# A hybrid layer on one core: no products with the zero state, and another order at both ends

## The chip, the core and the metric

The kernel runs on one core of a Trainium2 chip. The metric is the device time of one execution in microseconds. TensorE (PE) multiplies matrices, VectorE (DVE), ScalarE (ACT) and GpSimd (POOL) do the elementwise work, and SyncE (SP) issues most of the DMAs. Each engine works through its own instructions in the order in which they were written into its program, and waits on semaphores for the others. A difference of some 0.2% (2.6 us) is about what runs of this kernel can tell from none.

## The reference

One layer over 1024 frames of width 1024, in float32:

```
u = RMSNorm(h);  p = u @ W_in                      # q,k,v of attention; q,k,v, gate, decay, beta of the DeltaNet
A = chunked band attention (8 heads of 64)
B = gated DeltaNet (4 heads of 128), a recurrence over chunks:
      v_new = val - kc @ S
      o     = qd @ S + att @ v_new
      S     = S * cd + kt^T @ v_new                # S starts at zero
h = h + concat[RMSNorm(A), B] @ W_out
h = h + relu(RMSNorm(h) @ W1)^2 @ W2
```

S is the state. In the first chunk both products with S are zero and S times its decay is zero too. After the last chunk nothing reads S any more.

## The kernel before

Every float32 matrix is split into a high and a low part in a format that PE multiplies faster (line 147 casts the high part on ACT, line 148 subtracts it on DVE or POOL), and a product is three products of the parts.

The stages follow one another on PE: the projections of the DeltaNet (0 to about 235 us), of attention (to about 363), then attention together with the recurrence (to about 575), the output projection (to about 662), and the two layers of the feed-forward part, ff1 (to about 970) and ff2 (to 1281).

*The start.* GpSimd writes a matrix of ones. PE multiplies it with itself WARM times (line 111, tile warm), which is work for nothing but to keep PE busy. Meanwhile x and the gains (mgain) arrive. `load_xt` (lines 176 to 196) makes the high part uh of x times its gain on ACT (line 185), the low part ul on DVE (186), and squares x on ACT (190, 192) for the norm. ACT has to load a table before its first ACTIVATE, and the load stands in ACT's order just ahead of that instruction. `load_w` fetches the weights wdk of the first product, dk, and splits them.

*The recurrence.* The frames are eight chunks of 128 (c = 0 to 7), and each piece of a chunk is a generator that gives up its turn at every `yield`: `delta_prep` solves the triangular system and writes k with its tail decay (kt) to DRAM; `delta_state` forms tpv (v turned), pk (k times the state), pv (the new values vn), pq (q times the state, o) and pS (the update of the state); `delta_out` forms tpq, mt, po and the norm of o, whose reciprocal root is a chain of small operations on POOL (lines 131 to 143, with the power at 133); `delta_fin` turns o (tpo) and writes it, times the gate, into a quarter buffer mixd. Four-product groups go through `four` (line 461), turns through `four_t` (465). The state alternates between two tiles, the first of which is set to zero on POOL (line 231).

`interleave` mixes these pieces with the units of attention by weights, and the framework's planner then puts each engine's instructions into an order by priority and by its own estimate of times; buffers come from pools, and who gets one depends on that order. So the program order at one place can change when instructions are taken out at another.

*ff2.* The product of f and W2 is made with seven products in place of eight per block, in four blocks kb. Each product is 48 matmuls: `product` splits two operands of two tiles each (four splits on DVE), PE multiplies, and `accumulate` adds the result out of PSUM into one of seven sums y1 to y7 on DVE (line 1251), or copies it on ACT in the first block. The `prep` functions form sums and differences of operands on DVE in place, so their order matters. In the last block (`last`) the sums are also merged into the four quarters of the output (line 1255, on POOL or DVE), which `store` sends out. The very last product is made by rows (`by_rows`), so that each of its four results can be subtracted (line 1310) and sent out as soon as it is done; a row takes six matmuls with the first pair of operand tiles and then six with the second.

Of the kernel before, what the change touches and what calls it, by code (L numbers as in the profile page):

```python
# [8 lines left out]
F32 = mybir.dt.float32  # L9
F32R = mybir.dt.float32r  # L10
AF = mybir.ActivationFunctionType
# [24 lines left out]
ORDER = "OSMOSMFSOMOSMSL"  # L36
LATE = 2
SPREAD = 5
WARM = 8
LAST = {"b22": "t1", "t3": "t2", "t4": "b22"}  # L40
RS = "a"
NV = 6
# [4 lines left out]
def hymba_kernel(  # L47
# [53 lines left out]
    def bank(pool, name):  # L101
        return pool.tile([P, 512], F32, tag="bk", name=name)
# [3 lines left out]

    ones = cpool.tile([P, P], F32, name="ones")
    nc.gpsimd.memset(ones, 1.0)
    warm = bank(ps_o, "warm")
    for i in range(WARM):  # L110
        nc.tensor.matmul(warm[:, 0:P], ones, ones, start=True, stop=True)
# [64 lines left out]
    def load_xt(hf, k):  # L176

        raw = page("dk", f"xt{hf}{k}")
        if not hf and not k:
            nc.scalar.dma_start(out=raw, in_=x_t[0, :, 0:TH])  # L180
            nc.sync.dma_start(out=mgain, in_=mix_gain)
        else:
            nc.sync.dma_start(out=raw, in_=x_t[k, :, hf * TH:(hf + 1) * TH])
        hi, lo = u[hf][k]
        nc.scalar.mul(hi, raw, mgain[:, k:k + 1])
        nc.vector.scalar_tensor_tensor(lo, raw, mgain[:, k:k + 1], hi.bitcast(F32), ALU.mult, ALU.subtract)
        acc = squares[hf][k % 2]
        if acc is None:
            squares[hf][k % 2] = acc = page("pp", f"xs{hf}{k}")
            nc.scalar.activation(acc, raw, AF.Square)  # L190
        else:
            nc.scalar.activation(raw, raw, AF.Square)
            (nc.gpsimd if k % 2 else nc.vector).tensor_tensor(acc, acc, raw, ALU.add)

    for k in range(NKT):
        if k:
            w_dk.append(load_w(w_in[k * P:(k + 1) * P, DK:DK + 512], f"wdk_{k}"))
        load_xt(0, k)
        if not k:
            w_dk.append(load_w(w_in[0:P, DK:DK + 512], "wdk_0"))  # L200

    def row_load(src, w, name):
        t = mpool.tile([P, w], F32, name=name)
# [24 lines left out]
    split(wab, wab2[:, :, 0:8], wab2[:, :, 8:16], nc.scalar, nc.vector)  # L228

    state = [mpool.tile([P, 4, P], F32, name=f"state{i}") for i in range(2)]  # L230
    nc.gpsimd.memset(state[0], 0.0)

    q_dr = dram.tile([NT, 64, 2, 2, 512], F32, name="q_dr")
    k_dr = dram.tile([4, 2, P, SEQ], F32, name="k_dr")
# [256 lines left out]
    def delta_prep(kT, ab):  # L491
# [4 lines left out]
        for c in range(NT):  # L496
            n = f"d{c}"
            h4 = slice(4 * c, 4 * c + 4)
            tp = bank(ps_d, n + "_tp")
            four_t(tp, head(kT[c]))  # L500
            ss = sumsq(page("pp", n + "_sq"), "p", tp, n)
            kt = page("pp", n + "_kt")
            nc.vector.tensor_tensor(b4(kt), b4(tp), bc_row(ab["edec"][:, 1, h4]), ALU.mult)
            nc.sync.dma_start(out=kt_dr[c], in_=kt)
            yield 500
            L = decay("pp", n + "_L", ab, h4, tri_s, tri_ur, nc.vector)
            r = rsqrt("p", ss, 4, 1.0, EPS, n)
# [13 lines left out]
            nc.sync.dma_start(out=a_dr[c], in_=A)  # L521
            yield 900
# [74 lines left out]

    def delta_state(c, ab, kTs, Ys, D):

        n = f"c{c}"  # L600
        T = "wh" if c + 1 < NT else "jv"
        h4 = slice(4 * c, 4 * c + 4)
# [12 lines left out]
        pk = bank(ps_d, n + "_pk")  # L615
        four(pk, lambda h, hs: kT[:, hs], lambda h, hs: S[:, h, :])
        for h in range(4):
            hs = slice(h * P, (h + 1) * P)
            nc.vector.scalar_tensor_tensor(
                rr[:, hs], pk[:, hs], ab["nbr"][:, 4 * c + h:4 * c + h + 1], rr[:, hs],  # L620
                ALU.mult, ALU.add)
        yield 900
# [6 lines left out]
        pq = bank(ps_d, n + "_pq")  # L629
        four(pq, lambda h, hs: dq[:, hs], lambda h, hs: S[:, h, :])  # L630
        o = page("cv", n + "_o")
        nc.vector.tensor_tensor(b4(o), b4(pq), bc_row(ab["edec"][:, 0, h4]), ALU.mult)
        yield 900
        pS = bank(ps_d, n + "_pS")
        four(pS, lambda h, hs: ktail[:, hs], lambda h, hs: vn[:, hs])
        for h in range(4):
            nc.vector.scalar_tensor_tensor(
                S2[:, h, :], S[:, h, :], ab["edec"][:, 2, 4 * c + h:4 * c + h + 1],
                pS[:, h * P:(h + 1) * P], ALU.mult, ALU.add)
        D[c] = dq, dg, vn, o  # L640
        yield 900

    def delta_out(c, ab, kTs, D):
# [23 lines left out]
        nc.vector.tensor_tensor(o, o, po, ALU.add)  # L667
# [491 lines left out]
    def ff2(psw, pools):  # L1159
# [52 lines left out]
        for kb in range(nb):  # L1212
# [69 lines left out]

            accumulate(1, product(f"p1{kb}", lambda i: (a11[i], b11[i])))
            accumulate(5, product(f"p5{kb}", prep5))
            accumulate(2, product(f"p2{kb}", lambda i: (a12[i], b21[i])))
            if last:
                merge(nc.gpsimd, 2, 1)
                store(y[2], 0, 0)
            accumulate(3, product(f"p3{kb}", prep3))
            accumulate(6, product(f"p6{kb}", prep6))  # L1290
            if last:
                merge(nc.vector, 6, 1)
                merge(nc.gpsimd, 3, 5)
                for m in range(2):
                    nc.gpsimd.tensor_tensor(y[5][m], y[5][m], h11[m], ALU.add)
# [112 lines left out]
```

## Time and profile before

| | |
|---|---|
| time, median of 3 runs | 1288.59 us (1287.44 to 1289.28) |
| the profiled execution, its own time | 1288.31 us |
| its span | 1286.6 us |
| PE busy | 1260.6 us |
| DVE, ACT, POOL busy | 935.0, 553.9, 293.0 us |
| first product starts, last product ends | 6.30 us, about 1281.4 us |

The span is the time between the first and the last instruction that the profile shows; the execution takes 1.7 us more. In the profile a row gives the start, the duration, the engine, the line, the operation and the tiles, and in brackets how long the engine had been idle and whom it had waited for. A row of the view by groups gives the count, then the busy time, the mean of one in ns and the idle time ahead of them.

### The profile page before, as it was taken

How to read it: one execution, taken by the hardware profiler on the slowest of the kernel's cores; microseconds unless marked ns; L12 is line 12 of the kernel's file. 1: busy time of each engine (PE TensorE's matmuls, PEld its weight loads, DVE VectorE, ACT ScalarE, POOL GpSimd, SP SyncE). 2: the span in 40 equal slices, each digit the busy share in tenths (PEclk: the TensorE clock that was granted, in tenths of full speed). 3: DMA queues.
4: the chain of work that ended last, by engine and by line, in shares of the span. 5: the costliest groups of instructions: out<-in, count | busy, mean ns of one | idle time of the engine just before them, and what ended most of it. 6: DMA issues, size and time to landing. Idle time of an engine off the chain costs nothing.

```text
span 1286.6 us, 18043 instructions
## 1 busy us (share of the span) xinstructions
PE 1260.6 (98%) x6702; PEld 1040.6 (81%) x6702; DVE 935.0 (73%) x1401; ACT 553.9 (43%) x919; POOL 293.0 (23%) x499
## 2 busy tenths in 40 slices
PE   9999999999999999989999999999999999999998
PEld 7778878788888887868877788888887888888886
DVE  7899987665046666863529876776668997897988
ACT  7233132133166664665335445444455443333331
POOL 4435461454024355523310000000000000000034
PEclk9999999999999999999999999999999999999999
DMA  6214353656492742125351433232358733422002
GB/s 223 61 44 140 100 164 112 145 147 160 144 270 79 218 109 75 42 65 163 122 166 31 151 116 129 98 110 97 105 196 318 238 93 104 131 86 95 17 33 98
DMA packets 129288, 160.65 MB, mean 125 GB/s; under 512 B 22832, under 2 KB 71984, under 8 KB 128688
## 3 DMA queue, kind: packets, MB, share of 16 engines
q1 hardware_dynamic: 111104, 137.20, 34.7%
q10 hardware_dynamic: 18096, 22.29, 5.0%
q8 instruction: 53, 0.87, 0.3%
q14 instruction: 35, 0.29, 0.1%
HBM read 111.75 MB, written 47.71 MB: 124 GB/s over the span
## 4 chain that ended last, share of the span: by engine, by line
PE 72%; DVE 8%; issue 2%; DMA 2%; POOL 1%; ACT 1%; POOLq 1%; SPq 0%; ACTq 0%; DVEq 0%
PE q L1087 22%; PE p L1183 20%; PE op L166 5%; PE av_ps L166 3%; PE aq_ps L166 3%; PE g_ps L166 3%; PE t_o L865 3%; PE ak_ps L166 2%; PE t_sb L793 1%; PE t_sa L793 1%; PE t_tpb L844 1%; PE t_tpa L855 1%; PE c_mt L461 1%; PE c_pS L461 1%; DVE ml L148 1%
## 5 line engine op out<-in xcount | busy, mean ns | idle before, releaser
L1255 POOL TENSOR_TENSOR y<-y,y 128x1024 f32<-128x1024 f32 x6 | 19.3, 3243 | 591.7 <-DVE y L1251 572.9
L1251 DVE TENSOR_TENSOR y<-y,p 128x1024 f32<-128x1024 f32 x46 | 55.2, 1218 | 5.4 <-PE p L1183 4.5
L808 DVE CUSTOM_DVE_ANT_0 t_pb<-t_sb,biasn 128x256 f32<-128x256 f32 (+1 forms) x64 | 25.4, 402 | 43.6 <-POOL biasn L720 25.4
L166 PE MATMUL op<-mh,wo_h 128*128 128x512 f32 x128 | 50.3, 393 | 0.8 <-DVE t_nm L808 0.3
L166 PE MATMUL op<-ml,wo_h 128*128 128x512 f32 x128 | 50.1, 391 | 0.0
L166 PE MATMUL op<-mh,wo_l 128*128 128x512 f32 x128 | 48.3, 391 | 0.0
L823 ACT ACTIVATE t_pb<-t_pb,t_nm 128x256 f32<-128x256 f32 (+1 forms) x64 | 31.6, 494 | 22.7 <-DVE t_nm L817 12.7
L966 DVE TENSOR_TENSOR h<-op,op_x 128x512 f32<-128x512 f32 x16 | 10.8, 688 | 30.7 <-PE op L166 30.7
L793 PE MATMUL t_sb<-ks,t_q 128*128 128x256 f32 (+1 forms) x144 | 30.4, 308 | 0.8 <-DMA t_q<-q_dr 0.5
L973 POOL TENSOR_TENSOR op_q<-op_q 128x512 f32<-128x512 f32 x14 | 20.1, 1439 | 48.0 <-ACT op_q L972 47.8
L166 PEld LDWEIGHTS op<-mh,wo_h 128*128 128x128 f32 x128 | 24.0, 188 | 7.4 <-issue 1.0
L817 DVE CUSTOM_DVE_ANT_0 t_pa<-t_sa,biaso,t_nm 128x384 f32<-128x384 f32 (+2 forms) x48 | 26.3, 547 | 4.4 <-PE t_sa L793 2.9
L865 PE MATMUL t_o<-t_ta,vt 128*64 128x128 f32 x240 | 27.3, 293 | 1.4 <-DVE t_ta L858 1.1
L166 PEld LDWEIGHTS op<-mh,wo_l 128*128 128x128 f32 x128 | 24.0, 188 | 5.2 <-issue 0.2
L166 PEld LDWEIGHTS op<-ml,wo_h 128*128 128x128 f32 x128 | 24.0, 188 | 4.9
L166 PE MATMUL g_ps<-uh,wg_h 128*128 128x512 f32 x64 | 25.2, 394 | 1.4 <-ACT wg_h L147 1.4
L826 ACT ACTIVATE t_pa<-t_pa,t_nm 128x384 f32<-128x384 f32 (+2 forms) x48 | 26.4, 550 | 0.1
L793 PE MATMUL t_sa<-ks,t_q 128*128 128x256 f32 (+2 forms) x128 | 25.5, 310 | 0.3 <-DVE t_nm L808 0.3
L166 PE MATMUL g_ps<-uh,wg_l 128*128 128x512 f32 x64 | 25.2, 394 | 0.4 <-POOL wg_l L148 0.4
L166 PE MATMUL dq_ps<-uh,wdq_h 128*128 128x512 f32 x64 | 25.5, 398 | 0.0
L166 PE MATMUL dv_ps<-uh,wdv_l 128*128 128x512 f32 x64 | 25.4, 397 | 0.0
L166 PE MATMUL aq_ps<-waq_h,uh 128*128 128x512 f32 x64 | 25.3, 401 | 0.0
(1102 smaller groups left out, 4353.8 us busy)
## 6 DMA issues: line engine op xcount, KB each, us to landing
wa<-in_w_ff_dram SPq DMA_DIRECT2D x32, 512.0 KB
a<-in_w_ff_dram SPq DMA_DIRECT2D x32, 512.0 KB
b<-f_dr SPq DMA_DIRECT2D x32, 512.0 KB
f_dr<-yy ACTq DMA_DIRECT2D x16, 512.0 KB
t_q<-q_dr SPq DMA_DIRECT2D x30, 256.0 KB
f_dr<-zz ACTq DMA_DIRECT2D x13, 512.0 KB
ks<-k_dr SPq DMA_DIRECT2D x16, 256.0 KB
wo_r<-in_w_out_dram SPq DMA_DIRECT2D x16, 256.0 KB
```

The source lines that it names most:

```text
L166: nc.tensor.matmul(ps, a, b, start=(i == 0), stop=(i == n - 1))
L461: nc.tensor.matmul(ps[:, hs], lhs(h, hs), rhs(h, hs), start=True, stop=True)
L793: nc.tensor.matmul(o, q[m][:, i * P:(i + 1) * P], k[:, c], start=(m == 0), stop=(m == 1))
L808: nc.vector.tensor_tensor_reduce(sb[:, c], bk[:, c], new[g][pp][:, c], -1.0, 3.0e38, ALU.add, ALU.min, nm[:, 4 + i:5 + i])
L817: nc.vector.tensor_tensor_reduce(sa[e][:, 0:wa], bk[:, 0:wa], old[g][i][:, 384 - wa:384], -1.0, nm[:, 4 + i:5 + i], ALU.add, ALU.min, nm[: ...
L823: nc.scalar.activation(sb[:, c], sb[:, c], AF.Exp, bias=m, scale=-1.0, accum_out=T["sums"][:, 4 + i:5 + i])
L826: nc.scalar.activation(sa[e][:, 0:wa], sa[e][:, 0:wa], AF.Exp, bias=m, scale=-1.0, accum_out=T["sums"][:, i:i + 1])
L865: nc.tensor.matmul(po[64 * e:64 * e + 64, pp * P:(pp + 1) * P], vt[k0 + j][:, 64 * h:64 * h + 64], (ta[e] if j < na else tb)[:, c:c + P], ...
L973: nc.gpsimd.tensor_tensor(acc, acc, sq, ALU.add)
L1087: nc.tensor.matmul(part(ps, q), l[:, s], r, start=(k + m == 0), stop=(k == 3 and m == 2))
L1183: nc.tensor.matmul(part(ps[q], 0) if by_rows else part(ps[q // 2], q % 2), l[:, s], part(r, k), start=(i + k + m == 0), stop=(i + k + m == 4))
L1251: nc.vector.tensor_tensor(y[i][m], y[i][m], ps[m], op)
```

## The change

1. WARM goes from 8 to 11. An ACTIVATE on a column of the ones (turn_on) is ScalarE's first operation, and the load of the first weights wdk_0 and their split are written between the split of x and its square.
2. In the recurrence's first chunk there are no products pk and pq; o is a copy of po, the state a copy of pS, and the state is not set to zero at the start. In the last chunk there is no product pS and no update, k's tail is not formed, stored or loaded.
3. In the last block of ff2 the products run 1, 5, 6, 7, 3, 2, 4 in place of 1, 5, 2, 3, 6, 7, 4. The sums 2 += 1, 3 += 5, y5 += h11, 3 += 6 and 5 += 7 are POOL's now, and y5, y3 and y2 are stored after products 7, 3 and 2.

```
-WARM = 8
+WARM = 11
...
     nc.gpsimd.memset(ones, 1.0)
+    turn_on = cpool.tile([P, 1], F32, name="turn_on")
+    nc.scalar.activation(turn_on, ones[:, 0:1], AF.Square)
...
         nc.vector.scalar_tensor_tensor(lo, raw, mgain[:, k:k + 1], hi.bitcast(F32), ALU.mult, ALU.subtract)
+        if not hf and not k:
+            w_dk.append(load_w(w_in[0:P, DK:DK + 512], "wdk_0"))
         acc = squares[hf][k % 2]
...
-    nc.gpsimd.memset(state[0], 0.0)
...
-            kt = page("pp", n + "_kt")
-            nc.vector.tensor_tensor(b4(kt), b4(tp), bc_row(ab["edec"][:, 1, h4]), ALU.mult)
-            nc.sync.dma_start(out=kt_dr[c], in_=kt)
+            if c + 1 < NT:
+                (the same three lines)
...
-        ktail = page("cv", n + "_kt")
-        nc.sync.dma_start(out=ktail, in_=kt_dr[c])
+        if c + 1 < NT:
+            (the same two lines)
...
+        if c:
             pk = bank(ps_d, n + "_pk")
             four(pk, lambda h, hs: kT[:, hs], lambda h, hs: S[:, h, :])
             (and its four updates of rr)
...
+        if c:
             pq = bank(ps_d, n + "_pq")
             four(pq, lambda h, hs: dq[:, hs], lambda h, hs: S[:, h, :])
             nc.vector.tensor_tensor(b4(o), b4(pq), bc_row(ab["edec"][:, 0, h4]), ALU.mult)
+        if c + 1 < NT:
             pS = bank(ps_d, n + "_pS")
             four(pS, lambda h, hs: ktail[:, hs], lambda h, hs: vn[:, hs])
+            if c:
                 (the four updates of S2)
+            else:
+                nc.vector.tensor_copy(S2, b4(pS))
...
-        nc.vector.tensor_tensor(o, o, po, ALU.add)
+        if c:
+            nc.vector.tensor_tensor(o, o, po, ALU.add)
+        else:
+            nc.vector.tensor_copy(o, po)
...
             def prep3(i):
+                if last:
+                    tt(s1[i], a12[i], s1[i], ALU.subtract)
+                    return s1[i], b22[i]
                 tt(s1[i], s1[i], a11[i], ALU.subtract)
                 tt(a12[i], a12[i], s1[i], ALU.subtract)
                 return a12[i], b22[i]

             def prep6(i):
+                if last:
+                    tt(s1[i], s1[i], a11[i], ALU.subtract)
                 tt(b11[i], b22[i], b11[i], ALU.subtract)
...
-            accumulate(2, product(f"p2{kb}", lambda i: (a12[i], b21[i])))
-            if last:
-                merge(nc.gpsimd, 2, 1)
-                store(y[2], 0, 0)
-            accumulate(3, product(f"p3{kb}", prep3))
-            accumulate(6, product(f"p6{kb}", prep6))
-            if last:
-                merge(nc.vector, 6, 1)
+            if not last:
+                accumulate(2, product(f"p2{kb}", lambda i: (a12[i], b21[i])))
+                accumulate(3, product(f"p3{kb}", prep3))
+                accumulate(6, product(f"p6{kb}", prep6))
+                accumulate(7, product(f"p7{kb}", prep7))
+            else:
+                merge(nc.gpsimd, 2, 1)
                 merge(nc.gpsimd, 3, 5)
                 for m in range(2):
                     nc.gpsimd.tensor_tensor(y[5][m], y[5][m], h11[m], ALU.add)
-                merge(nc.vector, 3, 6)
-                store(y[3], 0, 1)
-            accumulate(7, product(f"p7{kb}", prep7))
-            if last:
+                accumulate(6, product(f"p6{kb}", prep6))
+                merge(nc.vector, 6, 1)
+                merge(nc.gpsimd, 3, 6)
+                accumulate(7, product(f"p7{kb}", prep7))
                 merge(nc.vector, 7, 6)
                 merge(nc.vector, 4, 7)
                 merge(nc.gpsimd, 5, 7)
                 store(y[5], 1, 1, nc.scalar)
+                accumulate(3, product(f"p3{kb}", prep3))
+                store(y[3], 0, 1)
+                accumulate(2, product(f"p2{kb}", lambda i: (a12[i], b21[i])))
+                store(y[2], 0, 0)
             ps = product(f"p4{kb}", prep4, last)
```

The lines of the changed program are one to twenty-one higher than those of the program before (147 is 149, 461 is 462, 465 is 466, 1255 is 1268, 1251 is 1264).

The planner's order changes with it. PE's order in the recurrence, before, from the update of the state in one chunk (the names t_ are attention's, c_ and m_ the recurrence's):

```order
L592 MATMUL m_p_4286<-m_s_4062 64x64 x4
L461 MATMUL c_pS<-c_vn,c_kt 128x128 x4
L793 MATMUL t_sa_5499<-ks_3454,t_q 128x256 x2
L793 MATMUL t_sa_5499<-ks_3809,t_q 128x128 x2
L865 MATMUL t_o<-t_ta_5354,vt_3469 64x128
L793 MATMUL t_sa_5506<-ks_3456,t_q 128x256 x2
L793 MATMUL t_sa_5506<-ks_3811,t_q 128x128 x2
L477 MATMUL c_Ltd<-c_Ltg_4338,tri_sr 128x512
L478 MATMUL c_Ltd<-c_Ltg_4339,tri_sr 128x512
```

And now, from the update of chunk 3 to the po of the next, on the same engine:

```order
L462 MATMUL c_pS<-c_vn,c_kt 128x128 x4
L478 MATMUL c_Ltd<-c_Ltg_4539,tri_sr 128x512
L479 MATMUL c_Ltd<-c_Ltg_4540,tri_sr 128x512
L466 MATMUL c_tpv<-ident,c_jv 128x128 x4
L570 MATMUL m_p_4563<-m_yb,m_ab 32x32 x8
L466 MATMUL c_tpq<-ident,c_jq 128x128 x4
L462 MATMUL c_pk<-state_302,kT_658 128x128 x4
L579 MATMUL m_p_4605<-m_s_4530 32x32 x8
L466 MATMUL c_tpo<-ident,c_o 128x128 x4
L462 MATMUL c_pv<-c_jv,m_yb 128x128 x4
```

Before, rows of attention stand between all groups of the recurrence; now some 40 rows in a row, two and a half chunks, hold none.

POOL's order there, from one chunk's sum of squares (c_ss) to the root's last step:

```order
L682 TENSOR_TENSOR c_ss<-c_ss,c_q_4594 128x4
L562 MEMSET m_yb 128x512
L133 TENSOR_SCALAR c_v<-c_ss 128x4
L565 COPY m_yb<-m_s_4974 32x4x32 x3
L135 TENSOR_TENSOR c_y<-c_v,mhalf 128x4
L565 COPY m_yb<-m_s_4974 32x4x32
L660 TENSOR_TENSOR c_Lt<-c_Lt,tri_u 128x512
L138 TENSOR_TENSOR c_t<-c_y 128x4
L143 TENSOR_TENSOR c_t<-c_t,c_v 128x4
L144 TENSOR_SCALAR c_t<-c_t 128x4
L145 TENSOR_TENSOR c_r<-c_y,c_t 128x4
L684 TENSOR_TENSOR c_r<-c_r,c_qs 128x4
```

In two of these chunks the memset, the four copies and c_Lt stand inside the chain of the root.

DVE's order in the last block, from the accumulation of product 7, now:

```order
L1264 TENSOR_TENSOR y_0_9454<-y_0_9454,p_11300 128x1024
L1264 TENSOR_TENSOR y_1_9455<-y_1_9455,p_11301 128x1024
L1268 TENSOR_TENSOR y_0_9454<-y_0_9454,y_9453 128x1024
L150 TENSOR_TENSOR p23a_l<-a_3_11062,p23a_h 128x1024
L1268 TENSOR_TENSOR y_1_9455<-y_1_9455,y_9453 128x1024
L150 TENSOR_TENSOR p23b_l<-b_3_11066,p23b_h 128x1024
L1268 TENSOR_TENSOR y_9451<-y_9451,y_0_9454 128x1024
L1268 TENSOR_TENSOR y_9451<-y_9451,y_1_9455 128x1024
L150 TENSOR_TENSOR p43a_l<-a_3_11052,p43a_h 128x1024
L1298 TENSOR_TENSOR b_3_11066<-b_3_11046,b_3_11066 128x1024
L150 TENSOR_TENSOR p43b_l<-b_3_11064,p43b_h 128x1024
```

Before, product 7 was the last but one, and its merges stood behind all splits of p4; now they stand ahead of them, and 37 rows of this size stand from the accumulation of product 1 to the last split of p4.

More of the change, by code (lines that the diff above doesn't have):

```diff
@@ L198, in hymba_kernel @@
         load_xt(0, k)
-        if not k:
-            w_dk.append(load_w(w_in[0:P, DK:DK + 512], "wdk_0"))
     def row_load(src, w, name):
@@ L501, in delta_prep @@
             ss = sumsq(page("pp", n + "_sq"), "p", tp, n)
-            kt = page("pp", n + "_kt")
-            nc.vector.tensor_tensor(b4(kt), b4(tp), bc_row(ab["edec"][:, 1, h4]), ALU.mult)
-            nc.sync.dma_start(out=kt_dr[c], in_=kt)
+            if c + 1 < NT:
+                kt = page("pp", n + "_kt")
+                nc.vector.tensor_tensor(b4(kt), b4(tp), bc_row(ab["edec"][:, 1, h4]), ALU.mult)
+                nc.sync.dma_start(out=kt_dr[c], in_=kt)
             yield 500
@@ L607, in delta_state @@
             nc.sync.dma_start(out=b4(t), in_=src[c])
-        ktail = page("cv", n + "_kt")
-        nc.sync.dma_start(out=ktail, in_=kt_dr[c])
+        if c + 1 < NT:
+            ktail = page("cv", n + "_kt")
+            nc.sync.dma_start(out=ktail, in_=kt_dr[c])
         tp = bank(ps_d, n + "_tpv")
@@ L614, in delta_state @@
         yield 500
[L615 to L622, printed above, removed]
+        if c:
+            pk = bank(ps_d, n + "_pk")
+            four(pk, lambda h, hs: kT[:, hs], lambda h, hs: S[:, h, :])
+            for h in range(4):
+                hs = slice(h * P, (h + 1) * P)
+                nc.vector.scalar_tensor_tensor(
+                    rr[:, hs], pk[:, hs], ab["nbr"][:, 4 * c + h:4 * c + h + 1], rr[:, hs],
+                    ALU.mult, ALU.add)
+            yield 900
         pvn = bank(ps_d, n + "_pv")
@@ L628, in delta_state @@
         yield 900
-        pq = bank(ps_d, n + "_pq")
-        four(pq, lambda h, hs: dq[:, hs], lambda h, hs: S[:, h, :])
         o = page("cv", n + "_o")
[L632 to L639, printed above, removed]
+        if c:
+            pq = bank(ps_d, n + "_pq")
+            four(pq, lambda h, hs: dq[:, hs], lambda h, hs: S[:, h, :])
+            nc.vector.tensor_tensor(b4(o), b4(pq), bc_row(ab["edec"][:, 0, h4]), ALU.mult)
+            yield 900
+        if c + 1 < NT:
+            pS = bank(ps_d, n + "_pS")
+            four(pS, lambda h, hs: ktail[:, hs], lambda h, hs: vn[:, hs])
+            if c:
+                for h in range(4):
+                    nc.vector.scalar_tensor_tensor(
+                        S2[:, h, :], S[:, h, :], ab["edec"][:, 2, 4 * c + h:4 * c + h + 1],
+                        pS[:, h * P:(h + 1) * P], ALU.mult, ALU.add)
+            else:
+                nc.vector.tensor_copy(S2, b4(pS))
         D[c] = dq, dg, vn, o
```

## The prediction

> **What bounds the kernel now.** I read the page's first part, then the windows of the stretch where attention and the recurrence share the engines, then the order of time at the start and at the end. The page:
>
> ```profile
> span 1286.6 us, 18043 instructions
> ...
> PE 1260.6 (98%) x6702; PEld 1040.6 (81%) x6702; DVE 935.0 (73%) x1401; ACT 553.9 (43%) x919; POOL 293.0 (23%) x499
> ```
>
> TensorE (PE) is busy 98% of the span, so 26 us in all are not PE work, 5 of them after its last product and 2.5 before its first. Taking PE work out counts in full; a wait that PE did not have before counts in full too. Windows of 10 us (PE, PE loads, DVE, ACT, POOL busy, granted clock, DMA):
>
> ```profile
> 440.00:450.00 10.00, 10.00 (x110) 9.23 (x109) 5.50 (x19) 7.22 (x23) 2.82 (x6) 1.00 0.57 173
> 480.00:490.00 10.00, 8.83 (x90) 7.20 (x89) 6.61 (x20) 4.38 (x14) 8.50 (x23) 1.00 0.02 5
> 500.00:510.00 10.00, 8.71 (x95) 7.62 (x94) 6.18 (x12) 3.65 (x9) 6.61 (x15) 1.00 0.23 57
> 540.00:550.00 10.00, 9.71 (x91) 8.12 (x90) 8.64 (x26) 6.62 (x19) 4.56 (x18) 1.00 0.01 2
> ```
>
> Where attention and recurrence alternate (440 to 450) PE never idles. Where almost only recurrence is left (480 to 490, 500 to 510) it idles 1.2 to 1.3 of 10 us; where only attention is left (540 to 550), 0.29. The mixing is what keeps PE full.
>
> **The work removed.** One group of four products with the state:
>
> ```profile
> L461 PE MATMUL c_pS<-c_vn,c_kt 128*128 128x128 f32 x64 | 9.2, 286 | 0.0
> L461 PE MATMUL c_pq<-state,c_jq 128*128 128x128 f32 x64 | 8.8, 280 | 0.0
> L461 PE MATMUL c_pk<-state,kT 128*128 128x128 f32 x64 | 8.6, 277 | 0.3 <-ACT m_s L570 0.3
> ```
>
> Each name has 64 passes in 8 chunks, so a group is busy 1.08 to 1.15 us; the passes overlap in their modelled ends, so three groups are worth 2.7 to 3.3 us of PE, I take **-2.8**. The four DVE updates, the copies put for the adds, one store and one load of k's tail and POOL's memset of the state are not on PE's way here, since DVE, ACT and the queues have idle time in that stretch (DVE 5.5 to 8.6 of 10 us above): nothing, and under 1 us if that cover were gone.
>
> **The start.** In order of time:
>
> ```profile
> 1.05 3.78 PE L111 MATMUL warm<-ones 128*128 128x128 f32 x16 [1.05 <-POOL ones L108]
> 3.20 1.28 ACT L185 ACT_TABLE_LOAD   x1 [3.20 <-DMA mgain<-in_mix_norm_gain_dram]
> 5.65 1.12 ACT L147 CAST wdk_h<-wdk_r 128x512 fp32r<-128x512 f32 x2
> 6.30 0.79 PE L307 MATMUL dk_ps<-uh,wdk_h 128*128 128x512 f32 x1 [1.47 <-ACT wdk_h L147]
> ...
> 9.45 0.63 PE L307 MATMUL dk_ps<-ul,wdk_h 128*128 128x512 f32 x1
> 9.88 1.46 PE L307 MATMUL dk_ps<-uh,wdk_l 128*128 128x512 f32 x4
> 11.17 1.07 PE L307 MATMUL dk_ps<-uh,wdk_h 128*128 128x512 f32 x4
> ```
>
> The table load waits for the gains' DMA and holds ACT until 4.48. With turn_on it starts when the ones are written, about 1.0, and is over by 2.3: uh starts at 3.2, wdk_h some 1.28 us earlier than 5.65. The warm matmuls take 0.47 us each, eleven of them 5.2 us, until 6.25: now they stand in front of the first product, which moves from 6.30 to 5.9-6.25, a gain of 0.05 to 0.4. But PE no longer idles 1.47 us before it. Products are 0.43 apart until 9.88 (half rate) and 0.23 to 0.32 from then on; if the full rate comes as soon as the warm matmuls end, 3.6 us at half rate become 1.8. So the start gives 0 to -2.2, I take **-1.3**: the clock opening about half as late as that. Data for the following products come earlier by the same 1.28 on ACT.
>
> The Trainium skill, TensorE: Matmul & The Clock Gate, Part 1: The HAM clock gate, says that the half rate ends after a busy window of about 3.4 us in a free-running grid, whose phase differs from run to run. The trace agrees in the half-rate spacing; by that rule the full rate would come anywhere from 4.5 to 7.9 and the start would give about 0.9 to 2.2.
>
> **The recurrence runs ahead alone.** The new program order moves more than the diff. After chunk 3's update, 40 rows on PE, three transposes c_tpo among them, hold recurrence work only, since the planner holds tiles 4 and 5 of attention behind chunk 4's mixd. What decides there is how soon PE's c_tpo of a chunk follows its c_po. Rows of one pass in the present trace (PE: the first, the last and the two longest waits), and of the operations between the two:
>
> ```profile
> 498.36 0.47 PE L477 MATMUL c_Ltd<-c_Ltg,tri_sr 128*128 128x512 f32 x1
> ...
> 503.58 0.43 PE L577 MATMUL m_p<-m_s 32*32 32x32 f32 x8 [0.53 <-DVE c5q_ss L488]
> 504.43 0.43 PE L577 MATMUL m_p<-m_s 32*32 32x32 f32 x8 [0.41 <-ACT m_yb L578]
> ...
> 510.16 1.06 PE L461 MATMUL c_pq<-state,c_jq 128*128 128x128 f32 x8
> ```
>
> ```profile
> L667 DVE TENSOR_TENSOR c_o<-c_o,c_po 128x512 f32<-128x512 f32 x8 | 5.5, 687 | 10.3 <-PE c_po L461 10.3
> L486 ACT ACTIVATE c_po<-c_o 128x512 f32<-128x512 f32 x8 | 4.8, 601 | 4.5 <-DVE c_o L667 4.5
> L488 DVE TENSOR_REDUCE c_ss<-c_po 128x4 f32<-128x512 f32 x8 | 5.5, 687 | 1.2 <-ACT c_po L486 1.1
> L133 POOL TENSOR_TENSOR c_y<-c_v,mhalf 128x4 f32<-128x4 f32 x8 | 8.3, 1033 | 0.7
> L141 POOL TENSOR_TENSOR c_t<-c_t,c_v 128x4 f32<-128x4 f32 x8 | 1.6, 198 | 0.6
> L650 POOL TENSOR_TENSOR c_Lt<-c_Lt,tri_u 128x512 f32<-128x512 f32 x8 | 10.6, 1328 | 5.6 <-ACT c_Lt L480 5.5
> L563 POOL COPY m_yb<-m_s 32x128 f32<-32x128 f32 x32 | 9.1, 286 | 6.2 <-DMA m_s<-y_dr 4.8
> L560 POOL MEMSET m_yb<- 128x512 f32 x8 | 4.2, 526 | 14.9 <-PE m_p L592 14.5 <-ACT t_pb L884 0.4
> ```
>
> From the end of c_po: add 0.69, square 0.60, the multiply of c_pq that stands between on DVE, sum 0.69, with hand-overs about 2.5. On POOL the power 1.03, seven small steps at 0.28 apart (2.0), and in the new order the memset 0.53, four copies (1.14) and c_Lt 1.33 stand between them: 6.0. Then 0.7 to 0.8 on DVE (same row form as the add). Together 9.3 after c_po's end. PE has c_pq, m_p, c_pS, c_Ltd, c_tpv, m_p, c_tpq, c_pk, m_p before c_tpo: the rows of the pass above, 12.9 us in all, hold about 1.6 of attention's transposes, 1.5 idle (four such waits) and 9.8 of work, of which some 6.5 stand there. So PE waits up to 2.8 us in each of two passes, and in the third, where no copies or c_Lt stand in POOL's chain (about 3.2 there), about 0.5: 6.1. The present order pays 1.3 in its window 500 to 510 and 1.2 in 480 to 490, which the new one need not pay; I grant it 2.1 of them. Net about **+4.0**; bounds 0 (the copies and c_Lt are done before the sum arrives, then the chain is 6.4 and c_tpo finds it ready) and +7.5 (nothing is saved elsewhere, and attention alone then idles as at 540 to 550 for some 50 us more, 1.4).
>
> **The last block.** The present end:
>
> ```profile
> 1216.55 2.35 DVE L1251 TENSOR_TENSOR y<-y,p 128x1024 f32<-128x1024 f32 x2
> 1244.62 1.21 DVE L148 TENSOR_TENSOR p73a_l<-a,p73a_h 128x1024 fp32r<-128x1024 f32 x1
> 1249.89 2.35 DVE L148 TENSOR_TENSOR p73a_l<-a,p73a_h 128x1024 fp32r<-128x1024 f32 x1
> 1258.85 3.43 DVE L148 TENSOR_TENSOR p43b_l<-b,p43b_h 128x1024 fp32r<-128x1024 f32 x1
> 1267.87 1.21 DVE L148 TENSOR_TENSOR p43b_l<-b,p43b_h 128x1024 fp32r<-128x1024 f32 x1
> 1273.54 4.62 DVE L1255 TENSOR_TENSOR y<-y,y 128x1024 f32<-128x1024 f32 x4
> 1281.39 0.69 DVE L1310 TENSOR_TENSOR y<-y,p 128x512 f32<-128x512 f32 x1 [1.45 <-PE p L1183]
> ```
>
> ```profile
> 1248.75 5.74 POOL L1255 TENSOR_TENSOR y<-y,y 128x1024 f32<-128x1024 f32 x2 [5.13 <-issue]
> 1254.45 6.74 POOL L1295 TENSOR_TENSOR y<-y,h 128x1024 f32<-128x1024 f32 x2
> 1274.89 7.85 POOL L1255 TENSOR_TENSOR y<-y,y 128x1024 f32<-128x1024 f32 x2 [13.70 <-DVE y L1255]
> ```
>
> ```profile
> 987.75 260.98 PE p L1183 x1150
> ```
>
> A split on DVE takes 1.14 (start to start) alone; the four from 1249.89 to the end of 1258.85's take 12.4 beside POOL's four merges: 7.8 lost, 1.95 per merge. Accumulations out of PSUM (2.35 for two) are not slowed. At present DVE starts the accumulation of p1 at 1216.55 and ends the last split of p4 at 1269.0; six merges fall in between, and it still idles 3 us there. In the new order 37 operations of that size stand from the accumulation of p1 to the last split of p4, 42.2 us, and all ten of POOL's merges are released in that time. Ten at 1.95 are 19; laid out one by one, with merges that fall beside PSUM operations free, 17.8. The last split ends at 1216.55 + 42.2 + 17.8 = 1276.5. PE wants it when six matmuls of p4 are done: 48 matmuls at 260.98 / 1150 = 0.227 are 10.9, so p4 runs from 1270.5 to 1281.4, and the six end at 1271.9. From 1276.5 the other 42 take 9.5: 1286.0, **+4.6** instead of 1281.4. DVE has 13.1 us of room, so this decides from 1.3 us per merge upward. Bounds: 0 (at 1273.54 DVE's merges took 1.16 each and POOL waited) and +13.6 (each merge costs DVE its whole 2.87, and the 17.8 grow to 26.7).
>
> The Trainium skill, SBUF, Who interferes with whom, calls the ports that VectorE and GpSimd share an exclusive lock on which the loser stands for the whole instruction. The trace agrees in kind (3.4 us for a split beside a merge, 1.14 alone); by it as stated DVE would lose up to a whole merge each time, 2.87 by the rows, and the sum would be 1301.
>
> **After the last product.** Now the store of y5 waits for POOL until 1282.74, 0.65 behind the last DVE row, with 1 MB before the end at 1286.6. In the new order only y4's four quarters of 256 KB are left there: -0.6 (0.65 of waiting) to -1.3 (and 256 KB less behind it), I take **-1.0**.
>
> **Sum** against the profiled execution, 1288.31 (0.28 under the median of 1288.59): -2.8 - 1.3 + 4.0 + 4.6 - 1.0 = +3.5, so 1291.8; with the median's offset 1292.
>
> **Rivals.** (1) *POOL loses the port, not DVE*: less than 1.3 us a merge, as in the row at 1273.54. PE never waits in the last block: 1288.6 + 3.5 - 4.6 = 1287.5, not slower. For it that DVE is first at the port when it works without a gap, as it will; against it the rows at 1249.89 to 1258.85, where DVE had work queued too. (2) *The recurrence alone costs nothing*: POOL's copies are done early, 1292 - 4 = 1288. For it the 6.4 of the bare chain against 6.5 of PE work; against it the window at 500 with most of those gaps. (3) *Both*: 1283.5, faster; the start and the removed products remain. (4) *Both losses at their upper bounds*: the recurrence costs 7.5 and the last block a whole merge each time: 1292 + 3.5 + 9 = 1304.5.
>
> **How the numbers follow.** A difference under 0.2% (2.6 us) can hardly be told from none here. Forecast 0.52 (1289 to 1296), rival 1 0.18, rival 2 0.15, rival 3 0.10, rival 4 0.05. Rivals 1 and 2 are mostly within 0.2%, rival 3 faster, a tenth of the forecast's case is within too, and a fifth of rivals 1 and 2 is faster: slower 0.52, same 0.32, faster 0.16. Predicted 1292; the range, 1284.5 to 1297.5, leaves out rival 3's lower half and all of rival 4.
>
> **What would show it.** Start: warm x22 without a gap before the first product, and 0.23 spacing before 9.4. Recurrence: PE waiting on DVE c_o before c_tpo, 2 to 3 us twice. Last block: splits of 2.4 to 3.4 from 1217 on, PE waiting for DVE p43b_l after six matmuls of p4, none of which exists now. If those splits take 1.2, or PE's idle between 363 and 575 is below its present 9, the forecast is wrong.

## The result

| | before | after |
|---|---|---|
| time, median of 4 runs | 1288.22 us (1287.44 to 1289.28) | 1317.96 us (1315.24 to 1318.98) |
| the profiled execution | 1288.31 us | 1315.24 us |
| its span | 1286.6 us | 1313.5 us |

The change makes the kernel 2.27% slower: the ratio is 1.0227, 95% interval 1.0212 to 1.0242. The forecast said slower, and 1292; the loss is 29.7 us, not 3.5. The traced execution of the changed kernel is the shortest of its four, with a mean granted clock of 0.993 against 0.989 to 0.991 in the others, so the trace has 26.9 us to explain.

The first part of the page after, its row of the granted clock included:

```profile
span 1313.5 us, 18001 instructions
...
PE 1269.5 (97%) x6684; PEld 1041.7 (79%) x6684; DVE 937.2 (71%) x1386; ACT 555.2 (42%) x920; POOL 295.1 (22%) x500
...
PEclk9999999999989999999999999999999999999998
```

PE's busy time grew by 8.9 us although it has 18 instructions less, and the span by 26.9: 18 us more of PE idle, and some PE work that ran slower. Where the stages end in the two traces tells where:

| PE's | before | after | shift |
|---|---|---|---|
| last dk_ps<-uh,wdk_h of line 307 (308 after) | 48.8 | 48.0 | -0.8 |
| last matmul of av_ps | 364.2 | 363.1 | -1.1 |
| first op<-mh,wo_l (output projection) | 573.5 | 593.4 | +19.9 |
| first product of ff2 | 969.5 | 988.3 | +18.8 |
| end of the span | 1286.6 | 1313.5 | +26.9 |

So attention with the recurrence lost 21.0 us, ff2 to the end 8.1, and the start won about 1. The first of these was priced at +4.0 less 2.8, the second at +4.6 less 1.0.

**The stretch of attention and recurrence, after.** Windows over it (PE, PE loads, DVE, ACT, POOL busy, granted clock, DMA share, GB/s), and two of its PE rows:

```profile
375.00:380.00 5.00, 3.17 (x18) 2.19 (x17) 1.02 (x6) 2.20 (x8) 1.80 (x2) 0.77 1.05 243
380.00:385.00 5.00, 5.00 (x32) 3.98 (x32) 1.50 (x7) 1.71 (x6) 1.14 (x4) 0.54 0.13 36
455.00:460.00 5.00, 4.92 (x35) 4.51 (x36) 1.72 (x3) 0.88 (x3) 4.42 (x10) 0.66 0.41 115
```

```profile
376.25 0.27 PE L868 MATMUL t_tpa<-ident,t_pa 128*128 128x128 f32 x1
378.35 0.77 PE L806 MATMUL t_sb<-ks,t_q 128*128 128x256 f32 x2 [1.83 <-DMA t_q<-q_dr]
```

At 376.25 PE runs out of work and waits for the queries t_q while the DMA engines are full (share 1.05). They were as full before (1.06 from 375 to 380) and PE did not wait, so why that load is late now is not shown. In the windows of and behind the wait the clock is granted at 0.77 and 0.54 of full speed, and once more at 0.66 at 455. What is missing of the clock in these windows comes to 5.2 us; the trace of before loses 1.7 in the same way at 553 to 557, so 3.5 of it is new. PE's idle time between 360 and 600 is 24.2 us against 8.7 before.

**The last block, after.** DVE, from the accumulation of p1 on, and POOL's merges:

```profile
1235.42 2.34 DVE L1264 TENSOR_TENSOR y<-y,p 128x1024 f32<-128x1024 f32 x2
...
1255.01 3.41 DVE L150 TENSOR_TENSOR p33a_l<-s,p33a_h 128x1024 fp32r<-128x1024 f32 x1
...
1265.08 1.21 DVE L150 TENSOR_TENSOR p33a_l<-s,p33a_h 128x1024 fp32r<-128x1024 f32 x1
1266.22 3.41 DVE L1268 TENSOR_TENSOR y<-y,y 128x1024 f32<-128x1024 f32 x1
...
1280.95 3.41 DVE L1268 TENSOR_TENSOR y<-y,y 128x1024 f32<-128x1024 f32 x1
...
1293.30 2.33 DVE L1264 TENSOR_TENSOR y<-y,p 128x1024 f32<-128x1024 f32 x2
1295.56 1.21 DVE L150 TENSOR_TENSOR p43a_l<-a,p43a_h 128x1024 fp32r<-128x1024 f32 x1
1296.69 1.21 DVE L150 TENSOR_TENSOR p43b_l<-b,p43b_h 128x1024 fp32r<-128x1024 f32 x1
...
1300.50 0.69 DVE L1331 TENSOR_TENSOR y<-y,p 128x512 f32<-128x512 f32 x1 [0.34 <-PE p L1196]
1304.38 0.69 DVE L1331 TENSOR_TENSOR y<-y,p 128x512 f32<-128x512 f32 x1 [3.20 <-PE p L1196]
...
1309.83 0.69 DVE L1331 TENSOR_TENSOR y<-y,p 128x512 f32<-128x512 f32 x1 [2.03 <-PE p L1196]
```

```profile
1236.77 5.75 POOL L1268 TENSOR_TENSOR y<-y,y 128x1024 f32<-128x1024 f32 x2 [551.83 <-ACT p63b_h L149]
...
1253.97 6.71 POOL L1312 TENSOR_TENSOR y<-y,h 128x1024 f32<-128x1024 f32 x2
1265.24 3.31 POOL L1268 TENSOR_TENSOR y<-y,y 128x1024 f32<-128x1024 f32 x1 [4.56 <-DVE y L1268]
```

What PE waited for from 1220 on (total, times, longest), and the clock in two windows of 4 us:

```profile
PE p L1196 <- DVE y L1264: 3.5, 1, 3.5
PE p L1196 <- DVE p23b_l L150: 1.5, 1, 1.5
PE p L1196 <- DVE p43b_l L150: 1.1, 1, 1.1
```

```profile
1295.00:1299.00 4.00, 2.94 (x10) 1.85 (x9) 4.00 (x5) 0.00 (x0) 0.00 (x0) 0.61 0.69 262
1299.00:1303.00 4.00, 4.00 (x11) 3.14 (x10) 1.85 (x3) 0.00 (x0) 0.00 (x0) 0.53 0.75 289
```

Splits and DVE's own merges take 3.4 us beside a merge of POOL, 1.2 beside none. PE waits three times, 6.1 us in all: 1.5 in product 2 for its split p23b_l (until 1285.55), 3.5 before p4 for the accumulation of product 3 (until 1294.65), and 1.1 within p4 for its last split, which ends at 1297.9. Behind the second of these waits the clock falls to 0.61 and 0.53 while p4's first rows run; behind the first it stays at 1.00 (1287 to 1291). From the last row of y4 to the end of the span it is 3.0 us in place of 4.5.

### The profile page after: what moved, and what is told of

Its sections match the earlier page's. It is cut to its first block, busy times and chain, and to the rows that moved or that the text cites. A ratio compares the mean times of both kernels' runs of the same rounds, so it can differ in the third digit from the quotient of the medians.

```text
span 1313.5 us, 18001 instructions
## 1 busy us (share of the span) xinstructions
PE 1269.5 (97%) x6684; PEld 1041.7 (79%) x6684; DVE 937.2 (71%) x1386; ACT 555.2 (42%) x920; POOL 295.1 (22%) x500
## 4 chain that ended last, share of the span: by engine, by line
PE 65%; DVE 13%; DMA 4%; issue 2%; ACT 2%; POOL 2%; SPq 0%; ACTq 0%; DVEq 0%; POOLq 0%
PE q L1100 21%; PE p L1196 15%; PE op L168 5%; PE aq_ps L168 3%; PE av_ps L168 3%; PE g_ps L168 3%; PE t_o L878 2%; PE ak_ps L168 2%; DMA t_q<-q_dr 1%; DVE y L1264 1%; PE t_sa L806 1%; PE t_sb L806 1%; PE t_tpa L868 1%; DVE y L1268 1%; PE t_tpb L857 1%
## 5 line engine op out<-in xcount | busy, mean ns | idle before, releaser
L1268 POOL TENSOR_TENSOR y<-y,y 128x1024 f32<-128x1024 f32 x8 | 24.6, 3085 | 571.5 <-ACT p63b_h L149 551.8
L806 PEld LDWEIGHTS t_sb<-ks,t_q 128*128 128x128 f32 x144 | 21.5, 195 | 6.3 <-issue 3.9
L860 ACT COPY t_tb<-t_tpb 128x512 f32<-128x512 f32 (+1 forms) x32 | 17.8, 555 | 18.4 <-PE t_tpb L857 18.3
L168 PE MATMUL aq_ps<-waq_l,uh 128*128 128x512 f32 x64 | 25.5, 399 | 0.0
```

Source lines behind the costliest of these rows:

```text
L168: nc.tensor.matmul(ps, a, b, start=(i == 0), stop=(i == n - 1))
L806: nc.tensor.matmul(o, q[m][:, i * P:(i + 1) * P], k[:, c], start=(m == 0), stop=(m == 1))
L1268: eng.tensor_tensor(y[i][m], y[i][m], y[z][m], ALU.add)
```

## The experiments

Each run is set against runs of the kernel before on the same chip; the ratio has its 95% interval and differs from that of the medians by up to 0.0006. The runs of this table come from three chips, so runs of different rows are compared by their ratios.

| run | edit | median, us | ratio | interval |
|---|---|---|---|---|
| e1_start | start alone | 1287.25 | 0.9999 | 0.9990 to 1.0008 |
| e2_state | recurrence alone | 1307.45 | 1.0153 | 1.0131 to 1.0176 |
| e3_ff2 | last block alone | 1294.75 | 1.0058 | 1.0043 to 1.0074 |
| e4_state_turns | e2, two yields kept | 1283.41 | 0.9970 | 0.9959 to 0.9982 |
| e5_turns_only | two yields out, all work kept | 1306.24 | 1.0148 | 1.0126 to 1.0170 |
| e6_ff2_no_merges | e3 without POOL's merges | 1285.93 | 0.9986 | 0.9977 to 0.9996 |
| e7_ff2_merges_on_dve | e3, merges on DVE | 1286.64 | 0.9990 | 0.9979 to 1.0001 |
| e8_all_mended | all three parts, e4's and e7's mends | 1281.09 | 0.9953 | 0.9936 to 0.9969 |
| e9_last_chunk | recurrence, chunk 7 alone | 1284.87 | 0.9977 | 0.9967 to 0.9986 |
| e10_third_bank | e2, merge products in attention's banks | 1292.06 | 1.0034 | 1.0021 to 1.0047 |
| e11_mended_third_bank | e8 with e10's banks | 1283.96 | 0.9974 | 0.9962 to 0.9986 |
| e12_mended_old_order | e8, ff2's products in the old order | 1282.31 | 0.9956 | 0.9940 to 0.9973 |

### The three parts alone

The start: the first four hunks of the diff, up to the second `load_w`, and no other.

> The kernel before with the start alone: eleven warm matmuls, turn_on, the first weights' load ahead of the square. By the trace of the changed kernel its projections end 1.1 us earlier (363.1 in place of 364.2), so 1287.1 if nothing takes that back: PE is never without work from there on. The rival, that the gain is lost because VectorE, nearly full between 40 and 180 us, is late instead, gives 1288.2. The order of every engine from the first product on is that of the kernel before.

Measured: no change, -1.3 to +1.0 us (1287.25, near the expected figure only because the kernel before has 1286.93 on this chip). The rows tell why the gain of one trace is not a gain of the kernel. PE's first products in e1 (new start), in e4 and in e3 (both with the start of before):

```profile
5.53 0.48 PE L309 MATMUL dk_ps<-uh,wdk_h 128*128 128x512 f32 x1
5.84 0.40 PE L309 MATMUL dk_ps<-ul,wdk_h 128*128 128x512 f32 x1
```

```profile
6.10 0.50 PE L306 MATMUL dk_ps<-uh,wdk_h 128*128 128x512 f32 x1 [1.42 <-ACT wdk_h L147]
6.44 0.39 PE L306 MATMUL dk_ps<-ul,wdk_h 128*128 128x512 f32 x1
```

```profile
9.30 0.53 PE L307 MATMUL dk_ps<-ul,wdk_h 128*128 128x512 f32 x1
9.67 1.08 PE L307 MATMUL dk_ps<-uh,wdk_l 128*128 128x512 f32 x4
```

e4 has the old start with its wait of 1.4 us for wdk_h, and yet runs at 0.23 us a product from its first one on; e3 and the kernel before run at 0.43 until 9.3 and 9.9. So the moment at which the full rate comes differs between executions of the same start. All five traces of the new start have the full rate from the first product, three of the nine of the old one do (e4, e5, e7). In the traces of the old start the matmuls of dk end between 47.7 and 49.5, in those of the new one between 47.7 and 48.0: the new start wins the worse part of that spread, 0.5 us on the mean, which is too little for the times to show. A wait of 0.6 to 1.0 us for VectorE's wdk_l near 17 us, which every trace with the full rate has under either start and no other has, takes back some of it.

The recurrence: the hunks on the state, from the memset to `delta_out`.

> The kernel before with the recurrence's part alone (no products with the state in chunk 0, no update in chunk 7). Theory: the whole loss between 363 and 594 us of the changed kernel, 21.0 us, comes from this part, because chunk 0 gives up its turn two times less and the planner then lets the recurrence run ahead of attention: 1288 + 20 = 1308 (1306 to 1311), with 48 rows of recurrence alone on PE and PE idle for over 10 us between 440 and 490. Rival: the lost time needs the other two parts (another phase of DMA and clock), then it is under +10.

Measured +19.7 us (17 to 23). This is the loss of the middle, and it needs neither of the other parts. The four executions differ: 1302.8 and 1305.0 us with a mean clock of 0.999, 1310.0 and 1310.7 with 0.993 and 0.991; the trace is of one of the first.

The last block: the hunks of `ff2`.

> The kernel before with the last block of ff2 in the new order alone. Theory: in the changed kernel the span from the first product of ff2 to the end grew from 317.1 to 325.2 us; that is all of this part's: 1288.2 + 8.1 = 1296.3 (1294.5 to 1298). PE waits some 6 us for VectorE before and in products 2 and 4, and p4 then runs its first rows at half rate. Rival: the last block is late only because the middle had shifted the DMAs of its operands; then it is under +2.

Measured +7.5 (5.5 to 9.5). The three parts add to 27, against 29.2 (27.3 to 31.2) for the change.

### Why the recurrence's part costs: the turns

```
-            yield 900          # in e2 both stand under "if c:"
+        yield 900              # e4: behind pk, and behind pq, for chunk 0 too
```

> The recurrence's part alone, but chunk 0 keeps the two yields that stood behind the products taken out, so it gives up its turn as often as before. No run of recurrence alone is left in PE's order. Theory (the turns, not the missing work, cost the time): 1288.2 - 2.8 for the removed products = 1285.4, within 1283.5 to 1288. Rival (the missing work itself lets chunk 0 and what follows arrive early and collide with the loads of attention's queries): over 1292.

Measured 1283.41, -3.9 us (2.3 to 5.3), a little under the expected range. The same products are left out, and 24 us come back. The longest run of recurrence on PE without a row of attention is 7 rows here and 8 in the kernel before, but 48 in e2 (441.6 to 488.0).

The twin: the kernel before, all work kept, without the two turns.

```
         rr[...] += pk * nbr
-        yield 900
+        if c:
+            yield 900
 ...
         o = pq * edec
-        yield 900
+        if c:
+            yield 900
```

> The kernel before with nothing but this: chunk 0 of the recurrence does not give up its turn behind pk and behind pq. All products and updates are still made. Theory (the two turns order the whole stretch): PE's order again has 49 rows of recurrence alone, and the time is that of the recurrence's part alone plus the 2.8 us of products that stay: 1287 + 20.5 + 2.8 = 1310 (1305 to 1313). Rival (the missing products and loads are needed for the loss): 1287, within 2.6.

Measured 1306.24, +19.1 (16 to 22). Nothing is missing from this kernel's work, and its longest run of recurrence is 49 rows (436.8 to 484.3), so the loss is one of order. And chunk 7's part alone, which leaves chunk 0 as it is:

> The recurrence's part for the last chunk alone: no product pS, no update and no store or load of k's tail in chunk 7, chunk 0 as before. Chunk 0's turns are untouched and PE's order has no run of recurrence alone. Theory (only chunk 0's turns cost): one product of about 1 us less, 1287 - 1 = 1286, same within 0.2%. Rival (the stretch loses whenever its instructions change at all): over 1292.

Measured 1284.87, -3.0 (1.8 to 4.3): faster by more than the one product (1.1) that is gone, so "same" was a miss. In the trace the stretch from av_ps to the output projection is 206.3 us against 209.3, 0.9 of it less idle time on PE and 1.1 the product; the last 1.0 may be the clock, since the 1.7 us that the trace of before loses at 553 to 557 are not lost in this one.

**What the order costs.** Three windows over the stretch, before and in e2 (PE, PE loads, DVE, ACT, POOL busy):

```profile
360.00:440.00 80.00, 80.00 (x767) 68.17 (x766) 46.96 (x161) 49.37 (x149) 29.79 (x80) 1.00 0.61 179
440.00:500.00 60.00, 57.60 (x556) 49.16 (x555) 38.10 (x121) 36.68 (x115) 28.80 (x77) 1.00 0.42 115
500.00:600.00 100.00, 93.72 (x724) 78.54 (x723) 66.13 (x162) 55.19 (x140) 43.80 (x98) 0.98 0.25 73
```

```profile
360.00:440.00 80.00, 77.69 (x735) 65.35 (x733) 43.76 (x147) 47.28 (x146) 30.95 (x84) 0.98 0.55 162
440.00:500.00 60.00, 48.43 (x473) 41.12 (x472) 32.58 (x75) 20.98 (x51) 31.89 (x78) 1.00 0.31 99
500.00:600.00 100.00, 89.84 (x737) 72.16 (x734) 65.36 (x201) 67.26 (x200) 31.44 (x85) 1.00 0.23 64
```

PE's idle time grows by 2.3 us in the first, mostly for t_q, by 9.2 in the second, where recurrence stands alone, and by 3.9 in the third, where attention is left alone. The wait for t_q is not the turns' doing: e4 has one of 1.2 us at the same place and loses nothing, and e5 has none there and loses as much. One pass of the recurrence alone, in e2:

```profile
445.34 0.68 PE L592 MATMUL m_p<-m_s 64*64 64x64 f32 x8 [0.78 <-DVE c_o L636]
445.94 1.16 PE L460 MATMUL c_pS<-c_vn,c_kt 128*128 128x128 f32 x8
...
448.25 0.66 PE L464 MATMUL c_tpv<-ident,c_jv 128*128 128x128 f32 x4 [0.69 <-ACT c_Lt L479]
...
449.62 0.43 PE L568 MATMUL m_p<-m_yb,m_ab 64*32 64x32 f32 x8 [0.34 <-ACT m_s L570]
...
452.78 0.43 PE L577 MATMUL m_p<-m_s 32*32 32x32 f32 x8 [1.22 <-DVE c_jv L622]
453.63 0.43 PE L577 MATMUL m_p<-m_s 32*32 32x32 f32 x8 [0.42 <-ACT m_yb L578]
454.07 0.63 PE L464 MATMUL c_tpo<-ident,c_o 128*128 128x128 f32 x4
...
460.41 0.67 PE L592 MATMUL m_p<-m_s 64*64 64x64 f32 x8 [0.78 <-DVE c_o L636]
461.01 1.16 PE L460 MATMUL c_pS<-c_vn,c_kt 128*128 128x128 f32 x8
```

A pass takes 15.07 us (445.94 to 461.01), 3.45 of it idle, in five waits. c_tpo, where the forecast put the wait, finds its operand ready. The three longest, m_p for c_o, m_p for c_jv and c_tpv for c_Lt, are waits for something that those products don't read: c_o is made from c_pq, c_jv from c_pk, c_Lt from c_Ltd, and with the reading of those a PSUM bank comes free. All of the recurrence's groups, the triangular merge's among them, take turns on the two banks of one pool. The run that gives the merge's products (m_p, m_tp) banks of another pool:

```
-        p1 = bank(ps_d, n + "_p1")
+        p1 = bank(ps_a, n + "_p1")     # the same for p2, tp and p4 of delta_merge
```

> The recurrence's part alone without the two turns, as in the run that lost 20 us, but the products m_p and m_tp of the triangular merge take their PSUM banks from the three of attention's scores, not from the two that all of the recurrence shares. Theory (where recurrence stands alone PE waits for one of two banks to be read): the planner, which counts those waits too, no longer leaves a run of recurrence alone, PE's waits on c_o, c_jv and c_Lt before m_p and c_tpv (7 us in all) go, and the time is 1284 to 1292. Rival (the two turns cost by letting the recurrence finish early, whatever the banks, so that attention is left alone at the end): 1300 or more.

Measured 1292.06, +4.4 (2.7 to 6.1): 15 us of the 20 come back without the turns, at the expectation's upper edge. What PE still waits for between 360 and 600, and two late windows:

```profile
PE t_sa L804 <- DVE t_nm L828: 2.4, 2, 2.2
PE m_p L592 <- ACT m_s L587: 0.3, 1, 0.3
```

```profile
500.00:520.00 20.00, 16.09 (x136) 12.56 (x132) 12.61 (x46) 11.94 (x42) 7.31 (x27) 1.00 0.20 53
560.00:580.00 20.00, 17.05 (x144) 12.83 (x144) 13.96 (x35) 11.81 (x32) 4.13 (x8) 1.00 0.22 73
```

The waits on c_o, c_jv and c_Lt are gone. But so is the run itself: the planner orders this kernel anew, and its longest run of recurrence is 5 rows in place of 48. So other banks for the merge take away the run of recurrence, as the kept turns do; that they would cure the waits within such a run is argued from the code and not shown. What remains are attention's own waits: from 500 to 600 PE idles 10.3 us, as in e2 (10.2) and more than before (6.3), which fits the rival for the rest.

### Why the last block costs: POOL's merges

Eight of the ten merges were POOL's before too; of the sums in the change's list only 3 += 6 is new to it. What the new order does is to bring all ten ahead of p4's last split, where six stood before (1237.87 to 1261.19 in the trace of before). e6 is e3 with these lines left out (three quarters of the output lack their merges):

```
-                merge(nc.gpsimd, 2, 1)
-                merge(nc.gpsimd, 3, 5)
-                for m in range(2):
-                    nc.gpsimd.tensor_tensor(y[5][m], y[5][m], h11[m], ALU.add)
...
-                merge(nc.gpsimd, 3, 6)
...
-                merge(nc.gpsimd, 5, 7)
```

> The new order of the last block alone, with POOL's ten merges left out, so three quarters of the output lack terms; VectorE's instructions are the same and in nearly the same order. Theory (VectorE is late because each merge on POOL holds it up for some 1.9 us): its 37 operations take 42 us, splits take 1.14 throughout, PE never waits in the last block and p4 runs at full rate: 1287 less 1.0 for the shorter end = 1286 (1284.5 to 1287.5). Rival (VectorE's four merges and the changed order of splits are late by themselves): over 1290.

e7 is e3 with `nc.vector` for `nc.gpsimd` in all of them.

> The new order of the last block alone, with POOL's ten merges on VectorE in place of GpSimd. Theory: a merge there costs VectorE 1.14, less than the 1.9 it costs it beside POOL; about 46 operations from the accumulation of p1 to the last split take 52.4, which ends at 1269 on the present time line, before PE wants it at 1271.9: no wait, 1285.5 to 1287.5. Rival (the number of operations ahead of the last split is what is too large, POOL or not): 10 x 1.14 more, over 1297.

Measured 1285.93 and 1286.64, against 1294.75 for e3. The last split of p4 in e6 and in e7:

```profile
1263.79 1.23 DVE L148 TENSOR_TENSOR p43b_l<-b,p43b_h 128x1024 fp32r<-128x1024 f32 x1
```

```profile
1269.05 1.25 DVE L148 TENSOR_TENSOR p43b_l<-b,p43b_h 128x1024 fp32r<-128x1024 f32 x1
```

Without the merges the last split begins at 1263.8; with all ten on DVE it begins at 1269.05 and ends some 1.3 us behind what was expected, still before PE wants it. PE waits for nothing in the last block of either. Ten more operations on the engine that was late cure it, because a merge takes 1.14 of DVE's own time and costs it about 2 when POOL does it: in the changed kernel DVE is busy without a break from 1235.42 to 1297.9, 62.5 us, of which 37 operations at 1.14 are 42.2, and the other 20.3 belong to ten merges. The two merges of 3 += 6 that changed engines are some 1.7 us of this, by an estimate from these figures (twice 2.0 less 1.14); no run takes them alone.

### What is worth keeping

e8 is the change with the yields of e4 and the merges of e7; e12 is e8 with ff2's products in the old order; e11 is e8 with the banks of e10.

> All three parts, with chunk 0's two yields kept and the last block's ten merges on VectorE. If the parts add up: start -0.3 (what its own run leaves room for), recurrence -3.5, last block -0.5 to -1: 1287 - 4.5 = 1282.5 (1281 to 1284). If either mend fails beside the other parts it is over 1287.

> The mended kernel, but the products of ff2's last block in the order of before, with the merges on VectorE all the same: what the new order is worth once the merges are not on GpSimd. Theory: nothing but the 0.6 to 1.3 us at the end, when the last stores are smaller: 1281.1 + 1 = 1282 (1280.5 to 1283). Rival (the merges' engine makes all of it): 1281.1.

> The mended kernel (all three parts, two turns kept, merges on VectorE) with the banks of the run above. It loses no run of recurrence now, so the theory leaves little to win: 1281, within 2.6. If scores of attention lack a bank, it is slower: up to 1288.

e8 is the fastest kernel here, 1281.09 us, 0.47% (0.31 to 0.64) under the kernel before. The new order of products by itself is worth 0.4 us by the ratios of e8 and e12, which the two intervals don't separate from none. More banks for the merge cost e11 2.7 us by the ratios, again with overlapping intervals, and its median lies 0.4 above the range of the theory, on the rival's side: there was no run of recurrence left to cure.

## Why the prediction was right or wrong

*The side* was right, the size was not: 1292 was forecast, range 1284.5 to 1297.5, and 1318 came. The step that failed most is the term +4.0 for the recurrence that runs ahead alone: it sought one wait, at c_tpo, where PE never waited, and the stretch lost 21.0 us, or 23.8 with the 2.8 of removed work that it hides. Step by step:

- **The work removed, -2.8.** Borne out in sign where the order is kept, and rather too small: e4 is 3.9 us faster, e9 with one of the three products 3.0.
- **The start, -1.3.** Too much: 0.0 (-1.3 to +1.0). The step took the half rate until 9.88 of one execution as a property of the old start. e4, e5 and e7 have that start and no half rate.
- **The recurrence runs ahead alone, +4.0, bounds 0 to 7.5.** The mechanism, PE starved where recurrence stands alone, was right and its place (chunks 3 to 6) too; the size failed in three ways. First, the wait was sought at c_tpo, by following data. PE waits in five other places, 2.7 us of it for the reading of groups that the waiting product does not use, which is a wait for their banks, and a pass has 3.45 us of waiting where the forecast had 2.8 (the work was right: 10.1 from c_Ltd to c_pq in e2, 9.8 forecast). Second, this was put at two full passes and a rest, net of 2.1 us for the waits it replaces, while PE's idle time grew by 9.2 in that window alone. Third, the two stretches around it were left out of the sum: 2.3 to 2.9 us of idle time, mostly for t_q, and 3.8 where attention is left with nothing beside it (the upper bound had 1.4 for that). "The new order need not pay" the old waits was a credit without a row.
- **The clock.** It had no term at all in the middle and in the last block. After: 0.77 and 0.54 behind the wait of 376, 0.66 at 455, 0.61 and 0.53 in p4. Worked out from windows of 5 us, each times what is missing of its clock, that is 5.2 us in the middle, 3.5 more than in the trace of before, and 2.4 in p4, which runs 11.9 us from its last split to its end (1309.8) where full rate gives 9.5. That work behind a wait can run at half rate stood in the first 10 us of the trace of before, and again at 553 to 557, and was used for the start alone.
- **The last block, +4.6.** Right in mechanism, and e6 and e7 prove it: DVE is held up by POOL's merges. From the accumulation of p1 to the end of the last split it took 62.5 us, not 60.0, and PE waited not for that split alone (1.1 us) but ahead of it for one of product 2 (1.5) and for the accumulation of p3 (3.5), which stands behind two splits of p4 on DVE; p4 does not read these sums, so what it waits for is taken to be their PSUM banks. With the clock the block's products end 9.6 us later, counted from the same accumulation, not 4.6.
- **After the last product, -1.0.** -1.5: 3.0 us from the last row to the end in place of 4.5. It does not need the new order: e12, with the old one and the merges on DVE, has 3.0 too.
- **The rivals.** None of the four came true. Rival 1 (POOL loses the port) and rival 2 (the recurrence alone costs nothing) are refuted by e6 and e5. Rival 4 pointed the right way with 0.05.

Of the middle's 21.0 us the trace gives 15.5 to idle time and 3.5 to the clock, less 2.8 for the products taken out. The last 5 are in PE's busy time and are not told apart.

The shared ports: the Trainium skill, SBUF, Who interferes with whom, calls the ports that VectorE and GpSimd share an exclusive lock, held for a whole instruction while the other engine stands. The trace agrees in kind: in the rows at 1255.01 to 1258.35 a split and a merge alternate at 3.4 us the pair, 1.14 of it the split's. A merge costs DVE 2.0 on the mean (20.3 for ten), not the whole 2.87 that a merge in a row takes: what runs beside a PSUM operation costs nothing, as forecast: the accumulation at 1235.42 takes 2.34 for two with POOL's merge of 1236.77 beside it, and 2.33 at 1293.30 with none.

## What to carry to other kernels

Taking work out of a generator also takes out its turns: when `yield`s set how streams are mixed, keep them where the work was (24 us lay between the two versions of one edit). Read the new order for stretches where one stream stands alone, and price such a stretch by the banks its groups share and by the clock behind each wait, not by its data alone. And an addition on an idle engine can cost the busy one more (2.0 us here) than doing it there (1.14), so look at which of them a new order brings ahead of work that is awaited.

## What was not expected of the hardware

Waits on PE are followed by work at half rate in some places and not in others, and the length of the wait alone does not tell which. Behind 1.8 us for t_q, until 378.35, the window from 380 to 385 has clock 0.54, and behind 3.5 and 1.1 us in the last block 1299 to 1303 has 0.53; behind 1.5 us in product 2 it stays at 1.00, and so it does in e12 from 380 to 385, behind a wait of 1.7 us for t_q. In e2 the recurrence's passes, each with 3.45 us of idle time in five pieces of at most 1.2, ran at 1.00 throughout 440 to 500; yet such passes have a window at 0.66 in the changed kernel (455 to 460) and in e5 (465 to 470). And executions with one and the same start (that of before) began with products 0.43 us apart in six traces and 0.23 in three.
